# A decoder trunk on one core: the two matmuls of every second weight block swap places

## The chip, the cores and the metric

The kernel runs on one core of one Trainium2 chip. The metric is the device time of one execution in microseconds. Three executions of the kernel before took 2417.88, 2414.39 and 2414.77 us; their median is 2414.77 us. One further execution was profiled; all rows below come from that one.

## The reference

Two layers over 256 tokens of width 2048. Layer 0 mixes tokens by a Conformer convolution module, layer 1 by chunked gated linear attention; each mixer is followed by a SwiGLU feed-forward network with an inner width of 5632. Cut to what the change touches (all in float32):

```
for i in range(2):
    mod = silu(c) @ w_ada[i] + b_ada[i]                  # shifts, scales and gates from a vector c
    h = rms_norm(x, pre_mix_g[i]) * (1 + sc1) + sh1
    y = conformer_conv(h, ...) if i == 0 else gla_mixer(h, ...)
    x = x + gt1 * rms_norm(y, post_mix_g[i])
    h = rms_norm(x, pre_ffn_g[i]) * (1 + sc2) + sh2
    gate, up = split(h @ w_in)                           # 2048 -> 2 x 5632
    y = (silu(gate) * up) @ w_out                        # 5632 -> 2048
    x = x + gt2 * rms_norm(y, post_ffn_g[i])
```

## The kernel before

Activations lie transposed: 128 channels on the partitions, the 256 tokens as columns. A product is a sum over weight blocks of 128 x 128: for output block `ob` and input block `k` the weight block is the stationary operand and the 256 token columns are streamed past it. To hold float32 accuracy in the faster fp32r format, each weight is split into a high and a low part (`hi`, line 326, a cast on ScalarE, ACT; `lo`, line 327, the rest, a subtraction on VectorE, DVE), and so is each activation (`x_hi`, `x_lo`). Three of the four partial products are summed: hi by x_hi, hi by x_lo and lo by x_hi.

`product` has three ways to do this for one block. The **wide** way, which the change touches, has `x_hi` and `x_lo` side by side in one operand of 512 columns. One matmul of 512 columns streams both past the high weights into all 512 columns of a PSUM bank (line 395); a second one of 256 columns streams `x_hi` past the low weights into the left 256 (line 398). When all blocks of an output block are summed, the right half is added to the left (`add_halves`, lines 409 to 411: a copy on ACT, a sum on DVE) or both halves are read one after the other. The **narrow** way takes three matmuls of 256 columns into one half bank (lines 392, 393, 398), for output blocks with a short tail. The **packed** way does the same with two output blocks in one bank (lines 368 to 370). Products: `pw2` (16 x 16 blocks, records named pw), `in` (feed-forward, first matrix, two layers and two halves), `out` (second matrix, the same), `wo`, `aqk`, `r`. The first eight output blocks of pw2, aqk and of the first half of `in` are packed; all of r and aqk, and the last output block of pw2, wo and the second halves of `out`, are narrow; the rest is wide. An output block takes 16 weight blocks in `in`, `wo` and `pw2` and 22 in `out`, one after the other (`block_order`).

Weights come in tiles of 16 blocks by DMA (`raw`, six buffers), and are split in halves of eight blocks; `hi` and `lo` have three buffers each, and `next_half` asks for the half that is three ahead. The cast of a later half therefore waits until the last matmul that reads the same `hi` buffer is done. Between these, DVE also does the conditioning products of `mod` (line 303).

The order of instructions on each engine is not that of the program: the build schedules by a simulated timeline, and may let a later matmul pass an earlier one whose operand it believes to be late. The calls that raise priorities (`high_priority`) and order by hand (`issue_after`) are not touched.

Of the kernel before, what the change touches and what calls it, by code (L numbers as in the profile page):

```python
# [17 lines left out]
T = 256  # L18
# [116 lines left out]
def trunk(ctx: ExitStack, tc: tile.TileContext, a: dict, out: bass.AP):  # L135
    nc = tc.nc
# [34 lines left out]
    for j in range(4):  # L171
        s = slice(j * 512, (j + 1) * 512)
# [165 lines left out]
    def next_half():  # L338
        i = state["used"]
        state["used"] += 1  # L340
        pump(i + ahead)
        run_waiting(i)
        return halves.pop(i)
# [6 lines left out]
    def product(name, kts, act, on_done, step=None, narrow=(), join=True, packed=0):  # L350
        live = {}
        seats = {}
        for ob, _ in ORDERS[name][:packed]:
            seats.setdefault(ob, divmod(len(seats), 2))
        banks, finished = {}, {}

        def done(ob, acc):
            on_done(ob, acc)
            if step is not None:
                step()  # L360

        def packed_block(ob, k, w_hi, w_lo, x_hi, x_lo):
            bank, half = seats[ob]
            if bank not in banks:
                banks[bank] = ps.tile([P, 512], F32, tag="mm", name=f"{name}_pair{bank}")
            acc = banks[bank][:, half * T : (half + 1) * T]
            opens, closes = k == 0 and half == 0, k == kts - 1
            nc.tensor.matmul(acc, w_hi, x_hi, start=opens, stop=False, skip_group_check=True)  # L368
            nc.tensor.matmul(acc, w_hi, x_lo, start=False, stop=False, skip_group_check=True)  # L369
            nc.tensor.matmul(acc, w_lo, x_hi, start=False, stop=closes, skip_group_check=True)  # L370
            if closes:
                finished.setdefault(bank, []).append((ob, acc))
                if half:
                    banks.pop(bank)
                    for pair in finished.pop(bank):
                        done(*pair)

        for idx, (ob, k) in enumerate(ORDERS[name]):
            if idx % HALF == 0:
                w_hi, w_lo = next_half()  # L380
            s = slice((idx % HALF) * P, (idx % HALF + 1) * P)
            pair = act(k)
            x_hi, x_lo = pair[:, 0, :], pair[:, 1, :]
            if ob in seats:
                packed_block(ob, k, w_hi[:, s], w_lo[:, s], x_hi, x_lo)
                continue
            if ob not in live:
                live[ob] = [ps.tile([P, 512], F32, tag="mm", name=f"{name}_{ob}"), 0]
            acc, n = live[ob]
            end = n == kts - 1  # L390
            if ob in narrow:
                nc.tensor.matmul(acc[:, :T], w_hi[:, s], x_hi, start=n == 0, stop=False)  # L392
                nc.tensor.matmul(acc[:, :T], w_hi[:, s], x_lo, start=False, stop=False)  # L393
            else:
                nc.tensor.matmul(  # L395
                    acc, w_hi[:, s], pair.rearrange("p a b -> p (a b)"), start=n == 0, stop=end, skip_group_check=True
                )
            nc.tensor.matmul(  # L398
                acc[:, :T], w_lo[:, s], x_hi, start=False, stop=end, skip_group_check=ob not in narrow
            )  # L400
            live[ob][1] = n + 1
            if end:
                live.pop(ob)
                done(ob, acc[:, :T] if ob in narrow else joined(ob, acc) if join else acc)
# [8 lines left out]
    def joined(ob, acc):  # L413
        t = tmp.tile([P, T], F32, tag="t", name=f"join{state['used']}_{ob}", bufs=TBUFS)
        add_halves(t, acc)
        return t
# [181 lines left out]
    for part in range(3):  # L598
        n = min(F_MAIN, F_COLS - part * F_MAIN)
# [110 lines left out]
    for idx, (c, k) in enumerate(PW1_CHUNKS):  # L710
# [3 lines left out]
        if idx % 2 == 0:  # L714
            w_hi, w_lo = next_half()
# [5 lines left out]
        s = slice(idx % 2 * WIDE, (idx % 2 + 1) * WIDE)  # L721
        for t in range(2):
            n = slice(t * P, (t + 1) * P)
# [55 lines left out]
    def pw2_done(ob, acc):  # L779
        gather(ob, "p", acc, kind=1, bias=col("conv_b_pw2", ob))  # L780

    product("pw2", KD, h_act, pw2_done, narrow=(KD - 1,), packed=HEAD * KD)

    def ffn(layer):
        with tc.tile_pool(name=f"ffn{layer}", bufs=1) as fp:
            m = fp.tile([P, KH, 2, T], F32R, tag="m", name=f"m{layer}")
            for half in range(2):
                gates = {}

                def in_done(ob, acc):  # L790
                    if ob < KF:
                        direct = half == 0 and ob < HEAD // 2
                        g = tmp.tile([P, T], F32, tag="t", name=f"gate{layer}_{ob}", bufs=TBUFS) if direct else acc
                        nc.scalar.activation(out=g, in_=acc, func=AF.Silu)
                        gates[ob] = g
                        return
                    i = ob - KF
                    g = gates.pop(i)
                    nc.vector.tensor_tensor(out=g, in0=acc, in1=g, op=ALU.mult)  # L799
                    split(g, m[:, i - half * KH, 0, :], m[:, i - half * KH, 1, :])  # L800

                product(f"in{layer}{half}", KD, h_act, in_done, packed=0 if half else HEAD * KD)

                def out_done(ob, acc):
                    yo = y[:, ob, :]
                    if half == 0:
                        add_halves(yo, acc)
                        if layer == 0:
                            gather_x(ob, f"f{layer}")
                        return  # L810
                    nc.vector.tensor_tensor(out=yo, in0=acc[:, :T], in1=yo, op=ALU.add)
                    if ob != KD - 1:
                        nc.vector.tensor_tensor(out=yo, in0=acc[:, T:], in1=yo, op=ALU.add)
                    gather(ob, f"f{layer}", yo, kind=4 * layer + 3, last=layer == 1)

                product(f"out{layer}{half}", KH, lambda k: m[:, k, :, :], out_done, narrow=(KD - 1,) if half else (), join=False)
# [6 lines left out]
    with tc.tile_pool(name="gla", bufs=1) as gp:  # L823
# [5 lines left out]
        with tc.tile_pool(name="scores", bufs=1) as sp:  # L829
# [80 lines left out]
            def step(n=1):  # L910
                for _ in range(n):
                    if work:
                        h, s = work.pop(0)
                        if s:
                            level(h, s)
                        else:
                            diagonal(h)
# [4 lines left out]
            for idx, (ob, k) in enumerate(ORDERS["v"]):  # L922
                if idx % HALF == 0:
                    w_hi, w_lo = next_half()
# [5 lines left out]
                s = slice((idx % HALF) * P, (idx % HALF + 4) * P)  # L930
# [162 lines left out]
```

## Time and profile before

| what | value |
|---|---|
| runs | 2417.88, 2414.39, 2414.77 us; median 2414.77 us |
| profiled execution, its own time | 2412.25 us |
| span from first to last instruction | 2410.5 us |
| mean granted TensorE clock over the span | 0.986 |
| PE busy | 2353.3 us, 14672 matmuls |
| PEld (weight loads) busy | 2051.8 us, 14672 loads |
| DVE busy | 1763.6 us |
| ACT busy | 1110.1 us |
| DMA | 605.27 MB, mean 251 GB/s |

Busy time counts each matmul from its start to a modelled end; since the next one starts before that end, the time that a matmul really costs is read from one start to the next. A stretch of matmuls of one kind without other work between them gives the same from its length and count; a window counts the instruction that is under way at its start too, so the number of starts is about one less than the count shown.

### The profile page before, as it was taken

To read this page: it belongs to the slowest core of one execution; us is meant where nothing else is said; L and a number is where in the kernel's file an instruction comes from. 1 tells how busy PE (TensorE), PEld (TensorE's weight loads), DVE (VectorE), ACT (ScalarE), POOL (GpSimd) and SP (SyncE) were. 2 spreads that over 40 slices of the span, in tenths; PEclk is the share of its full clock that TensorE was granted. 3 is DMA by queue.
4 is the path that set the end of the run, shared out by engine and by line. 5 is a ranking of instruction groups with operands and counts; after the bars stand their busy time and mean duration, and the time that the engine had idled before them with its cause. 6 is when DMAs were issued, how large, how long until landed. Compare 5 with 4: busy or idle time off the path is not lost.

```text
span 2410.5 us, 36312 instructions
## 1 busy us (share of the span) xinstructions
PE 2353.3 (98%) x14672; PEld 2051.8 (85%) x14672; DVE 1763.6 (73%) x2490; ACT 1110.1 (46%) x1659; POOL 23.9 (1%) x27
## 2 busy tenths in 40 slices
PE   7899999999999999999999999999999999999997
PEld 4677688998888888888899889989888888888886
DVE  5776669887776687779877978898666555666665
ACT  4333345554444444444455444454444444444442
POOL 0000000000000000000000000000000000000001
PEclk8999999999999999999999999999999999999998
DMA  9987978368777788778743666774565665665651
GB/s 390 392 341 277 345 272 336 134 244 300 287 286 285 290 307 293 292 283 295 269 158 127 245 253 252 283 274 140 204 216 209 222 217 208 224 214 208 223 184 65
DMA packets 85027, 605.27 MB, mean 251 GB/s; under 512 B 9574, under 2 KB 9958, under 8 KB 12022
## 3 DMA queue, kind: packets, MB, share of 16 engines
q1 hardware_dynamic: 84858, 602.95, 68.6%
q8 instruction: 115, 1.88, 0.3%
q14 instruction: 54, 0.43, 0.0%
HBM read 600.81 MB, written 2.10 MB: 250 GB/s over the span
## 4 chain that ended last, share of the span: by engine, by line
PE 94%; DVE 2%; DMA 2%; ACT 1%; issue 1%; POOL 0%; SPq 0%; POOLq 0%; ACTq 0%
PE in L395 25%; PE out L395 13%; PE in L398 12%; PE out L398 7%; PE pw L729 3%; PE pw L724 3%; PE pw L730 2%; PE wo L395 2%; PE r L392 1%; PE r L393 1%; PE r L398 1%; PE in_pair L369 1%; PE wo L398 1%; PE in_pair L368 1%; PE in_pair L370 1%; PE v L934 1%
## 5 line engine op out<-in xcount | busy, mean ns | idle before, releaser
L327 DVE TENSOR_TENSOR lo<-raw,hi 128x1024 fp32r<-128x1024 f32 x754 | 920.5, 1223 | 520.5 <-ACT hi L326 515.8
L326 ACT CAST hi<-raw 128x1024 fp32r<-128x1024 f32 x754 | 790.3, 1050 | 1048.9 <-issue 295.0
L395 PE MATMUL in<-h,hi 128*128 128x512 f32 x2560 | 900.1, 398 | 0.1
L398 PE MATMUL in<-h,lo 128*128 128x256 f32 x2560 | 716.7, 280 | 0.0
L395 PEld LDWEIGHTS in<-h,hi 128*128 128x128 f32 x2560 | 481.0, 188 | 117.8 <-DVE gate L799 0.3
L398 PEld LDWEIGHTS in<-h,lo 128*128 128x128 f32 x2560 | 483.4, 189 | 0.0
L395 PE MATMUL out<-m,hi 128*128 128x512 f32 x1364 | 477.3, 395 | 0.0
L398 PE MATMUL out<-m,lo 128*128 128x256 f32 x1408 | 392.2, 281 | 0.0
L303 DVE SCALAR_TENSOR_TENSOR raw<-raw,cb 128x2048 f32<-128x2048 f32 x160 | 365.2, 2284 | 12.1 <-DMA raw<-in_w_ada_dram 12.0
L395 PEld LDWEIGHTS out<-m,hi 128*128 128x128 f32 x1364 | 255.0, 188 | 58.4
L398 PEld LDWEIGHTS out<-m,lo 128*128 128x128 f32 x1408 | 264.4, 188 | 1.9
L724 PE MATMUL pw<-hi,h 128*128 128x512 f32 x256 | 101.3, 417 | 7.0 <-ACT h L467 6.7
L729 PE MATMUL pw<-lo,h 128*128 128x512 f32 x256 | 106.2, 417 | 1.2 <-DVE lo L327 1.2
L730 PE MATMUL pw<-hi,h 128*128 128x512 f32 x256 | 94.0, 395 | 0.0
L395 PE MATMUL wo<-oo,hi 128*128 128x512 f32 x240 | 83.7, 394 | 0.0
L398 PE MATMUL r<-h,lo 128*128 128x256 f32 x256 | 73.3, 286 | 0.0
L392 PE MATMUL r<-h,hi 128*128 128x256 f32 x256 | 73.2, 286 | 0.0
L393 PE MATMUL r<-h,hi 128*128 128x256 f32 x256 | 73.0, 285 | 0.0
L398 PE MATMUL wo<-oo,lo 128*128 128x256 f32 x256 | 71.2, 281 | 0.0
L369 PE MATMUL in_pair<-h,hi 128*128 128x256 f32 x256 | 70.9, 284 | 0.0
L370 PE MATMUL in_pair<-h,lo 128*128 128x256 f32 x256 | 68.9, 283 | 0.0
L368 PE MATMUL in_pair<-h,hi 128*128 128x256 f32 x256 | 68.0, 284 | 0.0
(363 smaller groups left out, 2939.1 us busy)
## 6 DMA issues: line engine op xcount, KB each, us to landing
raw<-in_in_dram SPq DMA_DIRECT2D x176, 1024.0 KB, 5.0
raw<-in_w_ada_dram SPq DMA_DIRECT2D x160, 1024.0 KB, 5.2
raw<-in_out_dram SPq DMA_DIRECT2D x88, 1024.0 KB, 5.0
raw<-in_pw_dram SPq DMA_DIRECT2D x48, 1024.0 KB, 7.7
raw<-in_w_ada_r_dram SPq DMA_DIRECT2D x32, 1024.0 KB, 8.3
raw<-in_aqk_dram SPq DMA_DIRECT2D x17, 1024.0 KB, 5.1
raw<-in_v_dram SPq DMA_DIRECT2D x16, 1024.0 KB, 5.0
raw<-in_r_dram SPq DMA_DIRECT2D x16, 1024.0 KB, 6.6
```

Source lines behind the costliest of these rows:

```text
L303: nc.vector.scalar_tensor_tensor(out=raw, in0=raw, scalar=1.0, in1=cb, op0=ALU.mult, op1=ALU.mult, accum_out=modcol(name, i))
L326: nc.scalar.copy(hi, part)
L327: done = nc.vector.tensor_tensor(out=lo, in0=part, in1=hi.bitcast(F32), op=ALU.subtract)
L369: nc.tensor.matmul(acc, w_hi, x_lo, start=False, stop=False, skip_group_check=True)
L370: nc.tensor.matmul(acc, w_lo, x_hi, start=False, stop=closes, skip_group_check=True)
L392: nc.tensor.matmul(acc[:, :T], w_hi[:, s], x_hi, start=n == 0, stop=False)
L393: nc.tensor.matmul(acc[:, :T], w_hi[:, s], x_lo, start=False, stop=False)
L395: nc.tensor.matmul(acc, w_hi[:, s], pair.rearrange("p a b -> p (a b)"), start=n == 0, stop=end, skip_group_check=True)
L398: nc.tensor.matmul(acc[:, :T], w_lo[:, s], x_hi, start=False, stop=end, skip_group_check=ob not in narrow)
L724: nc.tensor.matmul(accs[c][t], h_hi[:, k, n], w_hi[:, s], start=k == 0, stop=False)
L729: nc.tensor.matmul(accs[c][t], h_hi[:, k, n], w_lo[:, s], start=False, stop=False)
L730: nc.tensor.matmul(accs[c][t], h_lo[:, k, n], w_hi[:, s], start=False, stop=k == KD - 1)
```

## The change

The two matmuls of a wide block are put in a list. For odd blocks (the second, fourth, ... of an output block) the list is reversed: the one of 256 columns comes first. Operands, destinations and the number of instructions stay the same; `start` goes to the first matmul of an output block and `stop` to the last one. Written A for 512 and B for 256 columns, the program's order goes from A B, A B, A B, A B to A B, B A, A B, B A. Narrow blocks keep their order.

```diff
             acc, n = live[ob]
             end = n == kts - 1
+            parts = [(acc, w_hi[:, s], pair.rearrange("p a b -> p (a b)")), (acc[:, :T], w_lo[:, s], x_hi)]
             if ob in narrow:
-                nc.tensor.matmul(acc[:, :T], w_hi[:, s], x_hi, start=n == 0, stop=False)
-                nc.tensor.matmul(acc[:, :T], w_hi[:, s], x_lo, start=False, stop=False)
-            else:
+                parts = [(acc[:, :T], w_hi[:, s], x_hi), (acc[:, :T], w_hi[:, s], x_lo), parts[1]]
+            elif n % 2:
+                parts.reverse()
+            for i, (dst, weight, moving) in enumerate(parts):
                 nc.tensor.matmul(
-                    acc, w_hi[:, s], pair.rearrange("p a b -> p (a b)"), start=n == 0, stop=end, skip_group_check=True
+                    dst, weight, moving, start=n == 0 and i == 0, stop=end and i == len(parts) - 1,
+                    skip_group_check=ob not in narrow,
                 )
-            nc.tensor.matmul(
-                acc[:, :T], w_lo[:, s], x_hi, start=False, stop=end, skip_group_check=ob not in narrow
-            )
             live[ob][1] = n + 1
```

## Rows read from the trace of the kernel before

**Rows 1.** The page: busy time by engine, granted clock in 40 slices.

```profile
PE 2353.3 (98%) x14672; PEld 2051.8 (85%) x14672; DVE 1763.6 (73%) x2490; ACT 1110.1 (46%) x1659; POOL 23.9 (1%) x27
...
PEclk8999999999999999999999999999999999999998
```

**Rows 2.** The page: the chain that ended last, share of the span by engine.

```profile
PE 94%; DVE 2%; DMA 2%; ACT 1%; issue 1%; POOL 0%; SPq 0%; POOLq 0%; ACTq 0%
```

**Rows 3.** What PE waited for from 450 to 2392 us: total, times, longest.

```profile
PE aqk L398 <- DVE lo L327: 2.9, 2, 2.4
...
PE j_m L420 <- DVE f_xz L515: 1.1, 1, 1.1
```

**Rows 4.** Groups of PE instructions: the 512-column matmuls of the wide blocks.

```profile
L395 PE MATMUL in<-h,hi 128*128 128x512 f32 x2560 | 900.1, 398 | 0.1
...
L395 PE MATMUL out<-m,hi 128*128 128x512 f32 x1364 | 477.3, 395 | 0.0
...
L395 PE MATMUL wo<-oo,hi 128*128 128x512 f32 x240 | 83.7, 394 | 0.0
...
L395 PE MATMUL pw<-h,hi 128*128 128x512 f32 x112 | 40.7, 406 | 2.6 <-ACT y L506 2.6
```

**Rows 5.** Line 395 by stretch: length, PE busy (count), loads, clock, DMA.

```profile
500.00:700.00 200.00, 200.00 (x567) 106.43 (x567) 1.00 0.78 287
705.00:825.00 120.00, 119.62 (x342) 63.73 (x342) 1.00 0.79 287
850.00:1060.00 210.00, 210.00 (x607) 113.65 (x606) 1.00 0.80 295
1075.00:1180.00 105.00, 104.13 (x301) 55.56 (x300) 1.00 0.80 289
1546.00:1626.00 80.00, 79.71 (x230) 42.73 (x229) 1.00 0.77 284
2040.00:2260.00 220.00, 220.00 (x624) 117.12 (x623) 1.00 0.61 215
2274.00:2384.00 110.00, 109.85 (x316) 59.12 (x316) 1.00 0.42 144
```

**Rows 6.** Timeline of PE (start, us): matmuls of 256 columns alone, product r.

```profile
1500.96 0.28 PE L392 MATMUL r<-h,hi 128*128 128x256 f32 x1
...
1503.84 0.28 PE L392 MATMUL r<-h,hi 128*128 128x256 f32 x1
```

**Rows 7.** Timeline of PE: matmuls of 512 columns alone, product v.

```profile
1399.98 0.39 PE L935 MATMUL v<-hi,h 128*128 128x512 f32 x1
...
1402.02 0.39 PE L935 MATMUL v<-hi,h 128*128 128x512 f32 x1
```

**Rows 8.** Timeline of PE: wide blocks of `in`, layer 0, first half.

```profile
529.78 0.40 PE L395 MATMUL in<-h,hi 128*128 128x512 f32 x1
530.01 0.28 PE L398 MATMUL in<-h,lo 128*128 128x256 f32 x1
...
530.84 0.40 PE L395 MATMUL in<-h,hi 128*128 128x512 f32 x1
```

**Rows 9.** Timeline of PE: two places where the schedule swapped two matmuls.

```profile
713.51 0.62 PE L395 MATMUL out<-m,hi 128*128 128x512 f32 x2
713.97 0.40 PE L398 MATMUL out<-m,lo 128*128 128x256 f32 x2
714.21 0.39 PE L395 MATMUL out<-m,hi 128*128 128x512 f32 x1
...
1549.52 0.62 PE L395 MATMUL wo<-oo,hi 128*128 128x512 f32 x2
...
1550.21 0.40 PE L395 MATMUL wo<-oo,hi 128*128 128x512 f32 x1
```

**Rows 10.** The page: splitting the weights, mean ns of one, idle before.

```profile
L327 DVE TENSOR_TENSOR lo<-raw,hi 128x1024 fp32r<-128x1024 f32 x754 | 920.5, 1223 | 520.5 <-ACT hi L326 515.8
L326 ACT CAST hi<-raw 128x1024 fp32r<-128x1024 f32 x754 | 790.3, 1050 | 1048.9 <-issue 295.0
```

## The prediction

> **What bounds the kernel now.** I read the page's busy times first: PE is busy for 98% of the span and its clock is granted in full in nearly all slices [rows 1]. Busy time of matmuls overlaps, so the chain that ended last has to confirm it: 94% of that chain is PE [rows 2]. Then the waits of PE: from 450 to 2392 us there are three of them, the longest 2.9 us in total, the shortest 1.1 us, and none in a wide product [rows 3]. So in the wide products nothing but PE's own pace from one matmul to the next sets the time, and a change of order counts only through that pace, or by making something late that is not late now.
>
> How many blocks the change touches: 2560 in `in`, 1364 in `out`, 240 in `wo`, 112 in pw2 [rows 4]. The first three make 4164 blocks; half of each has its two matmuls exchanged.
>
> Next, what a block costs, by the views by stretch and in order of time. Each stretch's length over its count less one [rows 5] gives:
> - `in`, layer 0, first half (from 500 us): 200/566 = 353.4 ns.
> - `out`, layer 0, first half (705): 120/341 = 351.9 ns.
> - `in`, layer 0, second half (850): 210/606 = 346.5 ns.
> - `out`, layer 0, second half (1075): 105/300 = 350.0 ns.
> - `wo` (1546): 80/229 = 349.3 ns.
> - `in`, layer 1, second half (2040): 220/623 = 353.1 ns.
> - `out`, layer 1, second half (2274): 110/315 = 349.2 ns.
>
> The two stretches not shown, the first halves of layer 1, repeat those of layer 0 (353.3 and 351.9). The same pair of matmuls thus costs between 346.5 and 353.4 ns, by stage. Clock is 1.00 in all of them, and the DMA rate doesn't sort them (295 GB/s in the fastest, 287 and 215 in the slowest) [rows 5]. Weighted by blocks (1152 in first halves of `in`, 704 in each second half, 704 in first halves of `out`, 660 in second halves, 240 in wo) the mean is 1462.0 us / 4164 = 351.1 ns.
>
> Matmuls of one length show what the pair would cost with nothing added. In r 24 steps of 256 columns go from 1500.96 to 1503.84 us, 120 ns each [rows 6]. In v nine steps of 512 go from 1399.98 to 1402.02 us, 226.7 ns each [rows 7]. Together 346.7 ns: the fast stage has just this, and the mean has 4.4 ns more. Where it is lost can be seen in the order of time: in the slow stage A starts at 529.78 and B 0.23 us later; three blocks on, 530.84, so 1.06 us for three [rows 8]; the steps in between vary by some 8 ns in a rhythm that repeats every three blocks. The extra belongs to the change of length from one matmul to the next; streams of one length don't have it.
>
> **The change part by part.**
>
> *The order on PE.* Before, every step between matmuls of a wide product changes the length (A to B, B to A). After, in two blocks there is one A to B, one B to B, one B to A and one A to A; also across output blocks, since 16 and 22 are even. Nothing is added or removed: 4164 x 2 matmuls and as many loads stay. If the extra of 4.4 ns hangs on the steps that change length, half of it goes: 346.7 + 2.2 = 348.9 ns a block.
>
> The trace before holds small samples of the new order, because the schedule swapped matmuls in places of `out` and `wo`. There are five places with A, A, B, B, A. In the first, the two A start at 713.51 and the A after the two B at 714.21 us: 0.70 us for two blocks; the lowest, at 1549.52, takes 0.69 [rows 9], and the others, at 1553, 1906 and 2278 us, 0.70 or 0.71. Mean 0.699: 349.5 ns a block. That is a transient of two blocks in a stream of the old order, so it's weak, but it shows that neither A to A nor B to B has a stall. Between 348.9 and 349.5 I take 349.2. Gain: (351.1 - 349.2) x 4164 = 7.9 us. The ends for the range: the fast stage's 346.5 everywhere gains 4.6 x 4164 = 19.2 us; the slow stage's 353.4 everywhere loses 2.3 x 4164 = 9.6 us. The 112 blocks of pw2 lie between the same ends, at most 112 x 6.9 = 0.8 us; I set them to 0.
>
> [...]
>
> *Later release of `hi`.* The last reader of a half's `hi` buffer was the A of its eighth block, with a B behind; now it is the very last matmul. The cast into that buffer can start some 120 ns (one B) later, and the DVE subtraction behind it too; `lo` is freed one A (227 to 240 ns) earlier. Cast and subtraction take 1.05 + 1.22 us [rows 10], while two halves of 8 x 0.35 = 2.8 us each are still to be worked through before PE needs the pair: 5.6 - 2.3 = 3.3 us of slack. Cost 0. If that cover were gone, 0.12 us would be paid per half, of which there are 4164/8 = 520, some 62 us; but PE waits for no `lo` in any wide product now [rows 3]. ACT and DVE queue in order behind that cast; both have idle time (46% and 73% busy [rows 1]).
>
> *Later end of an output block.* The right half of the bank is complete one B (0.12 us) later, so the copy of `add_halves` may start later. The next output block takes 16 x 0.35 = 5.6 us in another bank; cost 0. The last output blocks in front of the norms are narrow and keep their order.
>
> *The schedule.* The build may again exchange matmuls where it thinks `lo` late. That yields a few more or fewer mixed pairs, in tens of 4164 blocks: below 0.2 us. A wholly other order of ACT and DVE work I can't exclude; PE's lack of waits covers it.
>
> **Sum.** Profiled execution 2412.25 - 7.9 = 2404.4 us. The median of the runs shown is 2.5 us above the profiled one (2414.77 - 2412.25), so I predict 2407 us. Five us are 0.2% here, about the least that a measurement of this kernel tells from no change.
>
> **The rivals.**
> 1. *Order-blind pace.* Each stage keeps its own mean whatever the order, 351.1 ns overall: 2414.8 us. For it: the same order gives 346.5 and 353.4 in two stages that differ in nothing that the views show, so something else chooses. Against it: streams of one length have none of the extra.
> 2. *The slow rhythm is caught (slower).* Place: all wide stages, the fast second half of `in` in layer 0 above all. Swaps put a stage in one of its rhythms; if the steady A B B A leads to the slow one, each block takes 353.4 ns: +9.6 us, 2424 us. It decides from 351.1 + 4.8/4164 = 352.3 ns a block. For it: the slow pace is what 1856 of 2560 blocks of `in` have. Against it: the five places stay under it.
> 3. *The fast rhythm everywhere.* 346.5 ns: -19.2 us, 2395.6 us. For it: one stage has it for 210 us without a break [rows 5]. Against it: the five places lie above.
> 4. *The schedule undoes the exchange.* Then the trace shows A B, A B as before; same time as rival 1 and counted there.
>
> **How the numbers follow.** Forecast (348 to 350 ns) 0.40, rival 3 0.15, rivals 1 and 4 0.26, rival 2 0.19. The bound of 0.2% lies at 349.95 ns; the forecast and rival 3 are faster: 0.55. Same 0.26, slower 0.19. The likeliest case's own range is 2402 to 2411. The range of 8 in 10 takes in the fast rhythm and part of the way to the slow one: 2394 to 2421.
>
> **What would show it.** By stretch of line 395: a count that gives 349 ns in every wide stage, with the differences between `in` of layer 0's two halves gone. In the order of time: A x2 and B x2 merged, A to A near 230 and B to B near 120 ns. The other stages (pw1, v, r, the junctions) unchanged. Wrong would be: a stage at 353 or above; waits of PE for `lo`; or single A and B still alternating.

## The result and the profile after

The changed kernel takes 2398.61 us (median of four runs, 2398.28 to 2399.87), the kernel before 2415.51 us in the same comparison: a ratio of 0.993, 95% interval 0.9913 to 0.9947. That is 16.9 us less; the forecast was 2407 us, a gain of 7.9 us. The direction was right, and the gain foreseen was under half of the one that came. The time lies inside the stated range of 8 in 10 (2394 to 2421 us), but outside the range given for the likeliest case (2402 to 2411 us).

PE bounds the kernel as before: it is 98% busy and makes up 93% of the chain that ended last. The page of the changed kernel, busy time and clock, answers to [rows 1]:

```profile
PE 2339.2 (98%) x14672; PEld 2044.2 (85%) x14672; DVE 1764.1 (74%) x2490; ACT 1109.9 (46%) x1659; POOL 23.9 (1%) x27
...
PEclk8999899999999999999999999999999999999998
```

Its waits of PE from 450 to 2392 us (total, times, longest) answer to [rows 3]:

```profile
PE aqk L397 <- DVE lo L327: 2.9, 2, 2.4
PE j_my L420 <- DVE s_y L484: 2.3, 1, 2.3
PE end_rb L446 <- DVE end_dg L435: 1.5, 1, 1.5
PE j_m L420 <- DVE f_xz L515: 1.1, 1, 1.1
PE ss_end L420 <- ACT f_y L502: 0.6, 1, 0.6
```

The two waits that are new to the list lie at the very end of the kernel (which now falls into this window); none is in a wide product. So the gain is in PE's pace. Both matmuls of a block now have one line, 397. The view by stretch of this line (length, PE busy with its count, loads, clock, DMA) answers to [rows 5]; a window counts up to two matmuls that are under way at its start, so a block takes the length over half of the count less two:

```profile
510.00:700.00 190.00, 190.00 (x1093) 165.76 (x1092) 1.00 0.80 294
710.00:820.00 110.00, 110.00 (x640) 96.79 (x639) 1.00 0.81 296
830.00:1065.00 235.00, 235.00 (x1351) 205.07 (x1350) 1.00 0.81 294
1075.00:1180.00 105.00, 105.00 (x610) 92.35 (x609) 1.00 0.81 295
1545.00:1625.00 80.00, 80.00 (x466) 70.43 (x466) 1.00 0.78 279
1700.00:1880.00 180.00, 180.00 (x1036) 157.04 (x1035) 1.00 0.62 216
2020.00:2250.00 230.00, 230.00 (x1323) 200.69 (x1322) 1.00 0.62 218
```

All four stages of `in` (from 510, 830, 1700 and 2020 us) now have one pace: 348.3, 348.4, 348.2 and 348.2 ns. Before they had 353.4, 346.5, 353.3 and 353.1 ([rows 5], the third from the prediction); the one fast stage became slower by 1.9 ns. `out` (710, 1075) has 344.8 and 345.4 ns, `wo` (1545) 344.8: 4 to 7 ns less than before. Block counts times differences: `in` 576 x (5.1 + 5.1) - 704 x 1.9 + 704 x 4.9 = 8.0 us, `out` 704 x 7.1 + 330 x (4.6 + 3.8) = 7.8 us, `wo` 240 x 4.5 = 1.1 us, together 16.9 us.

The order of time in `in` shows the new order on PE, merged by kind (answers to [rows 8]):

```profile
529.95 0.40 PE L397 MATMUL in<-h,lo 128*128 128x256 f32 x2
530.18 0.63 PE L397 MATMUL in<-h,hi 128*128 128x512 f32 x2
530.65 0.39 PE L397 MATMUL in<-h,lo 128*128 128x256 f32 x2
530.88 0.62 PE L397 MATMUL in<-h,hi 128*128 128x512 f32 x2
531.34 0.40 PE L397 MATMUL in<-h,lo 128*128 128x256 f32 x2
```

From 529.95 to 531.34 are four blocks, 1.39 us. The profiled executions differ by less than the runs, 2412.25 - 2398.28 = 14.0 us, because in the profile after the work ahead of everything that the change touches took longer: the first packed matmul of pw2 starts at 340.88 us before and at 345.12 after, the first of `in` at 452.32 and 456.50. One difference shows there: the mean granted clock from 200 to 300 us was 1.00 before and 0.91 after (the fifth digit of PEclk). In the profile after it was 0.50 from 252 to 268 us, where the one before has 1.00, and there matmuls of 512 columns start 0.43 us apart (four steps from 267.05 to 268.75 us), where they start 0.23 apart right behind it. PE was busy for 9.3 of the 10 us up to 250 us after and for all of them before. Why the clock fell is not shown. In the eleven profiles of the experiments the start of `in` lies between 450.8 and 460.3 us, whatever the kernel. A reader who compares kernels by span alone has these 10 us on top; hence the readings below go by the pace of a stage.

### The profile page after: what moved, and what is told of

It reads as the page before. It is cut to its first block, busy times and chain, and to the rows that moved or that the text cites. A ratio compares the mean times of both kernels' runs of the same rounds, so it can differ in the third digit from the quotient of the medians.

```text
span 2396.4 us, 36151 instructions
## 1 busy us (share of the span) xinstructions
PE 2339.2 (98%) x14672; PEld 2044.2 (85%) x14672; DVE 1764.1 (74%) x2490; ACT 1109.9 (46%) x1659; POOL 23.9 (1%) x27
## 4 chain that ended last, share of the span: by engine, by line
PE 93%; DVE 3%; DMA 2%; ACT 1%; issue 1%; POOL 0%; SPq 0%; POOLq 0%; ACTq 0%
PE in L397 37%; PE out L397 20%; PE r L397 4%; PE wo L397 4%; PE pw L729 2%; PE pw L724 2%; PE pw L730 2%; PE pw L397 2%; PE aqk L397 2%; PE in_pair L369 1%; PE in_pair L368 1%; PE in_pair L370 1%; PE v L934 1%; PE v L935 1%; PE v L933 1%; PE s L884 1%
## 5 line engine op out<-in xcount | busy, mean ns | idle before, releaser
L397 PE MATMUL in<-h,hi 128*128 128x512 f32 x2560 | 804.7, 395 | 0.1
L397 PE MATMUL in<-h,lo 128*128 128x256 f32 x2560 | 502.9, 278 | 0.0
L397 PE MATMUL out<-m,hi 128*128 128x512 f32 (+1 forms) x1452 | 438.8, 385 | 0.0
L397 PEld LDWEIGHTS in<-h,hi 128*128 128x128 f32 x2560 | 390.0, 189 | 0.3 <-DVE gate L799 0.3
L397 PE MATMUL out<-m,lo 128*128 128x256 f32 x1408 | 280.9, 279 | 0.0
L397 PEld LDWEIGHTS out<-m,hi 128*128 128x128 f32 x1452 | 223.8, 188 | 2.1
L397 PE MATMUL r<-h,hi 128*128 128x256 f32 x512 | 94.7, 285 | 0.0
L397 PEld LDWEIGHTS r<-h,hi 128*128 128x128 f32 x512 | 80.0, 192 | 0.1
L397 PE MATMUL wo<-oo,hi 128*128 128x512 f32 (+1 forms) x272 | 80.1, 378 | 0.0
L411 DVE TENSOR_TENSOR join<-in,join 128x256 f32<-128x256 f32 x160 | 66.9, 418 | 0.0
```

Of the source, the lines that this page charges most:

```text
L397: nc.tensor.matmul(dst, weight, moving, start=n == 0 and i == 0, stop=end and i == len(parts) - 1, skip_group_check=ob not in narrow,)
L411: nc.vector.tensor_tensor(out=dst, in0=acc[:, :T], in1=dst, op=ALU.add)
```

## Experiments

A is the matmul of 512 columns, B the one of 256. The theories are numbered in the expectations. Two questions stood: why the order moves the pace, and why `in` (348.3 ns) and `out` (345) differ now though their matmuls have the same shapes. As built, the tiles lie in each partition at these distances: the streamed operand of `in`, h, begins a whole multiple of 512 bytes from the weight tiles hi and lo; those of `out` and `wo`, m and oo, begin 320 bytes past one. (k steps 2048 bytes in h, a weight block 512, so a distance holds for all blocks.)

**Runs of four of one length.** The changed kernel, but

```diff
+        owed = []
...
-            elif n % 2:
-                parts.reverse()
+            else:
+                owed.append(parts)
+                if n % 2 == 0:
+                    live[ob][1] = n + 1
+                    continue
+                parts = [p[j] for j in ((1, 0) if n % 4 == 3 else (0, 1)) for p in owed]
+                owed.clear()
...
```

> The changed kernel with the wide matmuls issued for two blocks at a time, A A B B, then B B A A, so that runs of four of one length follow each other: a step that changes the length only every other block (changed kernel: one a block, kernel before: two). Theory 1, the number of length changes sets a block's time: before 353.3 ns in most of `in` and 351 in `out`, changed 348.3 and 345.2, so on a straight line about 345.8 in `in` and 342.3 in `out`, some 11 us less, 2387 us. Theory 2, long runs go to what streams of one length cost (226.7 + 120 = 346.7 ns): `in` falls by 1.6 ns, `out` and `wo` rise by 1.5 ns, net -2 us, 2397 us.

Measured: 2408.18 us, ratio to before 0.9973 (0.9959 to 0.9987). Both matmuls by stretch, `in` (515), `out` (715), `in` (835):

```profile
515.00:695.00 180.00, 180.00 (x1028) 157.40 (x1027) 1.00 0.79 292
715.00:815.00 100.00, 100.00 (x580) 87.69 (x579) 1.00 0.81 296
835.00:1060.00 225.00, 225.00 (x1286) 196.77 (x1285) 1.00 0.81 294
```

`in` takes 180/513 = 350.9 ns and 350.5 ns, `out` 346.0. Half as many length changes as in the changed kernel, and `in` is slower by 2.4 ns. Theory 1 falls: the number of length changes does not by itself set the time. Theory 2 falls for `in` too, which should have come down to 346.7; only `out` went where it said.

**The place of h alone.** The changed kernel with h moved by 64 bytes against the weights:

```diff
-    ab = const.tile([P, KD], F32, tag="ab", name="ab")
+    ab = const.tile([P, KD + 16], F32, tag="ab", name="ab")[:, :KD]
...
-    s_y = const.tile([P, T], F32, tag="s_y", name="s_y")
+    s_y = const.tile([P, T + 16], F32, tag="s_y", name="s_y")[:, :T]
```

> The changed kernel with the activation tile h alone moved: it begins 32 bytes past a multiple of 128 like the weight tiles hi and lo, and is put at 96 past, where the operands m and oo of `out` and `wo` lie now. Order unchanged. Theory 3, the place of the streamed operand against that of the weights makes the difference between `in` (348.3 ns a block) and `out` (345.2): `in` and pw2 fall to 345.2, -3.1 x 2672 = -8 us, 2390 us, `out` stays. Theories 1 and 2 (order and length alone): nothing moves, 2398.6 us, within 0.1%.

Measured: 2389.33 us, ratio 0.9899 (0.9863 to 0.9934). `in` (515, 835) and `out` (715):

```profile
515.00:695.00 180.00, 180.00 (x1040) 157.81 (x1039) 1.00 0.80 292
715.00:815.00 100.00, 100.00 (x581) 87.94 (x581) 1.00 0.83 300
835.00:1060.00 225.00, 225.00 (x1299) 197.35 (x1298) 1.00 0.80 295
```

`in` falls to 346.8 and 347.0 ns, `out` stays at 345.4. So the place counts, but the 345.2 of theory 3 is not reached. The streams of 256 columns alone, which read h too, get faster as well. In product r of this kernel, ten blocks from

```profile
1519.72 0.28 PE L397 MATMUL r<-h,lo 128*128 128x256 f32 x1
...
1523.26 0.28 PE L397 MATMUL r<-h,lo 128*128 128x256 f32 x1
```

take 3.54 us: 118.0 ns a matmul, where [rows 6] gave 120.

**All moved together.** The same first edit with 8 in place of 16 floats and no second one: h and everything behind it move by 32 bytes, from 32 past a multiple of 64 bytes onto one. Once on the changed kernel, once on the one before.

> The changed kernel with h and everything behind it (hi, lo, m, oo, raw) moved by 32 bytes, so that all begin on a multiple of 64 bytes instead of 32 past one. Theory 4, reads that straddle 64-byte lines cost the extra: `in`, `out`, and the streams of one length too fall below 345 ns a block and 120 ns a matmul of 256 columns, 2370 us or less. Theory 3 (place relative to the weights) and theories 1 and 2: nothing moves, 2398.6 us.

> The kernel before (A B, A B) with the same move of h and everything behind it by 32 bytes. Theory 4: the slow rhythm goes, 353.3 ns falls to 346.7 ns or less, and the change of order is then worth little: under 2397 us. Theories 1 to 3: the block keeps 353.3 and 346.5 by stage, 2415 us.

Measured: 2398.84 us (ratio 0.9933, 0.9909 to 0.9957) and 2413.58 us (0.9991, 0.9974 to 1.0007). With the changed order `in` (515) is

```profile
515.00:695.00 180.00, 180.00 (x1035) 157.05 (x1035) 1.00 0.80 290
```

It keeps 180/516.5 = 348.5 ns, `out` 345.4: theory 4 falls. The move of all by 32 bytes changed nothing, while the move of h against the weights did (346.8). (hi, lo, raw, m and oo move together, so the runs do not tell which of the tiles behind h the distance must be taken to.) The old order brought a surprise. Line 395 by stretch (A alone, count less one), the four stages of `in`:

```profile
515.00:695.00 180.00, 180.00 (x510) 95.74 (x510) 1.00 0.80 290
835.00:1060.00 225.00, 225.00 (x650) 121.70 (x650) 1.00 0.81 294
1710.00:1880.00 170.00, 170.00 (x492) 91.72 (x491) 1.00 0.62 218
2030.00:2260.00 230.00, 230.00 (x652) 122.31 (x652) 1.00 0.61 216
```

353.6, 346.7, 346.2, 353.3 ns: the third stage is fast, where it was slow in the first profile. Was that the move, or chance?

**The kernel before, profiled again.** No edit.

> The kernel before, unchanged, profiled once more. Theory 6, A B, A B can run in a fast (346.5 ns) and a slow rhythm (353.3 ns), and which one a stage of `in` falls into is settled anew in each execution: at least one of the four `in` stages has another rhythm than in the first profile (slow, fast, slow, slow). Rival, the place in the program settles it: the same four.

Measured: 2413.99 us, one execution. The four stages of `in`:

```profile
515.00:695.00 180.00, 180.00 (x511) 95.86 (x510) 1.00 0.79 288
835.00:1060.00 225.00, 225.00 (x650) 121.83 (x650) 1.00 0.80 295
1710.00:1880.00 170.00, 170.00 (x482) 90.47 (x482) 1.00 0.61 213
2030.00:2260.00 230.00, 230.00 (x665) 124.49 (x664) 1.00 0.62 216
```

352.9, 346.7, 353.4, 346.4 ns. The fourth stage was slow in the first profile (353.1 [rows 5]) and is fast here, in the same program. Theory 6 holds in this: in `in`, A B, A B has two rhythms some 7 ns apart, each kept for a whole stage, and which one a stage has is not settled by the program alone.

But it is not drawn afresh for each stage, as the traces of both executions show. From its first start to its last, `out` of layer 0 takes 123.8 us in its first half in both and 123.7 in its second, `wo` 89.5 in both. They part in the first half of `out` of layer 1. There the schedule had swapped matmuls (at 1982 us in the first profile, at 1987 in this one), and line 395 before and after that place reads, in the first profile,

```profile
1920.00:1980.00 60.00, 60.00 (x171) 31.95 (x170) 1.00 0.61 211
1990.00:2020.00 30.00, 30.00 (x87) 16.18 (x87) 1.00 0.59 205
```

and in this one

```profile
1925.00:1985.00 60.00, 60.00 (x173) 32.37 (x172) 1.00 0.60 208
1995.00:2025.00 30.00, 30.00 (x86) 15.96 (x86) 1.00 0.58 200
```

So `out` has two rhythms as well, 353 and 349 ns, and changes from one to the other at the swapped place: 352.9 to 348.8 ns in the first profile, 348.8 to 352.9 in this one. The `in` that follows is slow behind the 349 and fast behind the 353. The same holds in layer 0 of both profiles (352.9 ns, then fast) and in both layers of the old order with all moved (352.9, then fast; 348.8, then slow), six times out of six. That the one sets the other is not shown, but it looks as if a rhythm were handed on from stage to stage. Nor does the record say that both executions ran on one chip, so a difference between chips isn't ruled out.

**Is the order only a dodge of a bad place?** The kernel before with the edit of the second experiment, h moved by 64:

> The kernel before (A B, A B) with h alone moved by 64 bytes against the weights, as in the run that made the changed kernel's `in` 346.4 ns a block. Theory 5, the change of order only dodged a clash of the streamed h with the weights' place: with h moved the old order needs no dodge, `in` 346.5 ns in all four stages, 2399 us or less, and the order is worth under 2 us there; `out` and `wo` keep 349 to 352 ns. Theory 2, the order is worth the same wherever h lies: `in` stays about 5 ns a block above the changed order's 346.4, 2407 us.

Measured: 2416.58 us (ratio 1.0011, 0.9999 to 1.0023). `in`:

```profile
515.00:695.00 180.00, 180.00 (x510) 95.89 (x510) 1.00 0.80 290
835.00:1060.00 225.00, 225.00 (x638) 119.88 (x637) 1.00 0.79 288
1710.00:1880.00 170.00, 170.00 (x482) 90.53 (x481) 1.00 0.62 217
2030.00:2260.00 230.00, 230.00 (x652) 122.49 (x652) 1.00 0.61 214
```

353.2 to 353.6 ns in all four. Theory 5 falls: in this place the old order shows only the slow rhythm in this profile, and the order is worth 6.6 ns a block (353.4 against 346.8). Neither of the two times foreseen, 2399 and 2407 us, came. Moving h without the new order gains nothing.

**h placed as m and oo are.** The changed kernel with only `s_y` widened, by 48 floats, so that the weights move 192 bytes away from h:

> The changed kernel with the weights and everything behind h moved by 192 bytes, so that h lies to the weights just as the operands m and oo do (320 bytes past a multiple of 512). Theory 3 in full, the place of the streamed operand against the weights is all that sets `in` apart from `out`: `in` falls from 348.3 to 345.2 ns, 2640 blocks and more, and the streams of 256 columns alone (r) change with it; 2386 to 2388 us. Rival, the 64 bytes are all that counts: 346.4 ns as with h moved by 64, 2389 us.

Measured: 2386.09 us, ratio 0.9885 (0.9858 to 0.9912). `in` (515, 835) and `out` (715):

```profile
515.00:695.00 180.00, 180.00 (x1046) 158.40 (x1045) 1.00 0.80 294
715.00:815.00 100.00, 100.00 (x581) 88.00 (x580) 1.00 0.82 300
835.00:1060.00 225.00, 225.00 (x1306) 197.97 (x1306) 1.00 0.81 297
```

344.8 and 345.1 ns in `in`, 345.4 in `out`: the two are level, as theory 3 said. This is the fastest kernel of the study. It pays elsewhere: matmuls of 512 columns alone get slower in product v, where the weights are streamed past h. Twelve steps from

```profile
1403.07 0.39 PE L935 MATMUL v<-hi,h 128*128 128x512 f32 x1
...
1405.87 0.39 PE L935 MATMUL v<-hi,h 128*128 128x512 f32 x1
```

take 2.80 us, 233.3 ns each instead of 226.7 [rows 7], and v as a whole takes 110.8 us instead of 109.0.

**Two more distances.** The same edit with 8 floats (32 bytes) and with 80 (320 bytes):

> The changed kernel with the weights and everything behind h moved by 32 bytes against h. If what counts is that h and the weights are 64 bytes apart in 128: `in` stays at 348.3 ns. If any offset from a common place is enough: 346.4 ns or less.

> The changed kernel with the weights and everything behind h moved by 320 bytes: h lies 192 past a multiple of 512 to the weights (0 in the changed kernel, 448 with h moved by 64, 320 with 192). If a distance of 64 in 128 is what counts, `in` takes 198.6 to 199.6 us for 576 blocks, as at 448 and 320. If the distance in 256 counts, 192 is like 448 and gives 199.6 us.

Measured, one execution each: 2409.38 and 2387.23 us. The first two stages of `in`, with 32 bytes and then with 320:

```profile
515.00:695.00 180.00, 180.00 (x1026) 157.07 (x1026) 1.00 0.80 293
...
835.00:1060.00 225.00, 225.00 (x1282) 196.29 (x1282) 1.00 0.80 292
```

```profile
515.00:695.00 180.00, 180.00 (x1041) 157.86 (x1040) 1.00 0.80 292
...
835.00:1060.00 225.00, 225.00 (x1300) 197.43 (x1299) 1.00 0.81 295
```

351.6 ns in both stages with 32 bytes, neither of the two values foreseen: this distance is worse than none. With 320 bytes 346.5 and 346.7, as with h moved by 64, which fits the idea that the distance counts within 256 bytes.

**The old order in the best place.** The kernel before with `s_y` widened by 48 floats:

> The kernel before (A B, A B) with the weights and everything behind h moved by 192 bytes, the place in which the changed order has 345.1 ns a block in `in`. If order and place act each by itself: the old order stays in one of its two rhythms, 346.5 to 353.4 ns in each stage of `in` (199.6 to 203.5 us for 576 blocks, 243.9 to 248.6 us for 704), 2405 to 2416 us. If the place alone is the cure: 345 ns and under 2390 us.

Measured: 2417.07 us (ratio 1.0003, 0.9994 to 1.0013). The four stages of `in` take 353.6, 353.2, 170/488 = 348.4 and 349.0 ns; the first and the third:

```profile
515.00:695.00 180.00, 180.00 (x510) 95.68 (x510) 1.00 0.80 289
...
1710.00:1880.00 170.00, 170.00 (x489) 91.67 (x488) 1.00 0.63 220
```

So `in` has two rhythms here too, 353.4 and 349, the two that `out` has in the kernel before, whose operand lies at this distance. Place alone is no cure.

**B first throughout.** The changed kernel, but

```diff
-            elif n % 2:
+            elif n:
```

> The changed kernel, but with the 256-column matmul first in every block after an output block's first, so B A, B A: as many length changes as before, and no pairs of one length. If it is the alternation A B B A that counts: the two rhythms of the kernel before are back, 199.6 or 203.5 us in the first halves of `in`, 243.9 or 248.6 us in the second ones, 2405 to 2418 us. If it were enough that B comes first: the changed kernel's 200.5 and 245.0 us.

Measured, one execution: 2419.02 us. `in` (515, 835) and `out` (715):

```profile
515.00:695.00 180.00, 180.00 (x1021) 156.38 (x1020) 1.00 0.79 285
715.00:815.00 100.00, 100.00 (x571) 87.31 (x570) 1.00 0.79 289
835.00:1060.00 225.00, 225.00 (x1277) 195.53 (x1276) 1.00 0.80 292
```

353.3 and 352.9 ns, `out` 351.5: close to the slow rhythm of the old order. The alternation does it, not B going first. (The expectation says that no pairs of one length are left. That is not quite so: each output block still begins A B, so it has one B B, and one A A stands where the next one begins.)

## Why the prediction was right in sign and short in size

*PE's pace alone bounds the wide products:* right. Waits of PE are the same three to the tenth of a microsecond, plus the kernel's end. The later release of `hi`, the later end of an output block and the schedule were put at nothing; no new wait shows, so that stands. pw2's 112 blocks take 42.7 us from their first A to their last before and 43.0 after, which is next to nothing.

*Swapping removes part of the extra:* right in sign, but not for the reason given, so the sign was in part luck. The step that failed is the term "half of it goes: 346.7 + 2.2 = 348.9 ns a block", taken as 349.2. It measured 348.3 in `in` (near) but 344.8 to 345.4 in `out` and `wo` (far). The gain on those 1604 blocks is 8.9 us, where 1.9 ns each would have been 3.0; on the 2560 of `in` it is 8.0, where 1.9 ns each would have been 4.9, since their mean before lay above 351.1. Two things were wrong in the working:
- 346.7 ns, the sum of a 256 and a 512 step alone, was taken as the floor, "what the pair would cost with nothing added". It is no floor: r's step itself falls from 120 to 118.0 ns when h is moved. The trace before had it too: in the narrow block of `wo`, whose operand is oo, 42 steps of 256 columns go from 1628.94 to 1633.89 us, 118 ns each. And the sum does not bound the pair: with the weights moved by 192 bytes a step of 512 alone takes 233.3 ns (v), one of 256 at the same distance 118 (the narrow block of `wo`), 351 together, and A B B A takes 345.1.
- The extra was hung on the steps that change length. The run with half as many of those was slower in `in` (350.9 against 348.3 ns); that explanation falls. The five places with A, A, B, B, A [rows 9] showed that no single step stalls, as the text said, but two blocks inside a stream of the old order did not tell the steady pace of the new one. What such places do in `out` is to change the rhythm of the blocks behind them, as rival 2 put it: "Swaps put a stage in one of its rhythms".

One reading was off without harm: the first of the two stretches that are not shown gives 180/509 = 353.6 ns by the text's own rule, not 353.3; the starts over that whole stage give 353.3, so the mean stands.

*Rival 1* asked why two like stages differ, and said that "something else chooses". The program alone does not: its fourth `in` stage had the slow rhythm in one execution and the fast one in another. So the forecast's base, 351.1 ns, was one draw. By the two profiles a slow stage of `in` costs 576 or 704 x 7 ns, 4 to 5 us. The changed order has no such draw in the traces: in its six profiles with A B B A (as built, h moved, all moved, and the weights moved by 192, 32 and 320 bytes) the four stages of `in` agree within 0.5 ns. The spread of the runs is no measure of this. The four runs of the changed kernel lie within 1.6 us, but the four with the weights moved by 192 bytes lie between 2382.51 and 2390.72 us, and their time rises as the mean granted clock falls, from 0.991 to 0.984.

*Rival 2*, the slow rhythm caught for good, didn't come for A B B A; B A, B A comes close to it, and A B has it with h moved. *Rival 3* (2395.6 us) came nearer to the time than the forecast, by another way: not the fast rhythm everywhere, but 348.3 in `in` and less than the fast 346.5 in `out`.

What stays open: why the distance between operand and weights counts at all, why the new order has one rhythm, and what hands the old order's rhythm on. The views show when a matmul starts, not what it waits for inside PE. The distances that were run (changed order, bytes past a multiple of 512, h to weights: 0, 192, 320, 448, 480) give 348.3, 346.6, 345.1, 346.8 and 351.6 ns; that a rule in 256 bytes lies behind is argued from two of them, not shown.

## What to carry to other kernels

When one stream of matmuls runs without waits and still costs some per cent more in one stage than in another of the same shapes (here 353.4 against 346.5 ns a block), look at the steps between starts, profile the same kernel twice, and try both the order of unequal matmuls and the distance of the streamed tile from the weights. Here they acted together: order alone gave 0.7% (ratio 0.993), place alone nothing (1.0011 and 1.0003), both 1.15% (0.9885). And a floor worked out from streams of one length is itself a measurement in one place, not a bound: here it was 346.7 ns, and the pair came down to 344.8.

## What the runs showed of the hardware that was not expected

- An unequal pair of fp32r matmuls (512 and 256 columns, a weight load each; 256 columns alone take 120 ns a step in r, and 232 ns in float32, six steps of line 633 from 148.81 to 150.20 us in the kernel before) showed steady rhythms: 346.5 and 353.4 ns a block in `in` of the kernel before, 349 and 353 in its `out`, with a granted clock of 1.00. One program had either in the same stage (the fourth `in`: 353.1 and 346.4 ns in two executions), and in `out` of layer 1 the rhythm changed where two matmuls were swapped (352.9 to 348.8 ns in one execution, 348.8 to 352.9 in the other).
- The distance in a partition between h and the weight tiles moved the pace of A B B A in `in` by up to 6.5 ns of 345 (351.6 at 480 bytes past a multiple of 512, 345.1 at 320), with the same matmuls in the same order. It moved matmuls of 512 columns alone, in v, where the weights are streamed past h, the other way: 226.7 ns at 0 and 233.3 at 320. Moving both together by 32 bytes changed nothing (348.5 against 348.3).
